# Rotary tables on VectorE, an earlier key for the memory's norm, and products padded to 128 rows

## The chip, the cores and the metric

The kernel runs on one core of one Trainium2 chip. The metric is the device time of one execution in microseconds (us). The median of three runs of the kernel before is 687.25 us (686.97 to 688.6).

## The reference

The reference is a decoder trunk of two layers over one sequence of 256 tokens, 1024 channels wide, in float32. Each layer normalises x, projects it with one matrix (1024 x 8224) and feeds five groups of heads:

- A, sparse attention with eight heads of 64 channels and two key heads: a compressed branch (keys and values of 32 tokens each, one every 16 tokens, so 16 compressed positions), a selected branch and a window branch, merged by gates;
- B, a Mamba-2 scan with eight heads, whose decays are exponentials of differences of running sums;
- C, causal attention in a window of 128, with rotary positions on queries and keys and a learned sink a head;
- D, dilated attention in three patterns;
- M, cross-attention of four heads into 256 memory tokens. The memory is normalised with each layer's own weights.

```python
for layer in range(DEPTH):
    h = rms_norm(x, pre_norm[layer])
    proj = jnp.einsum('bsd,de->bse', h, w_in[layer])
    a_out = nsa_mixer(...)        # compressed values: p_c @ vc, with 16 rows
    b_out = ssd_mixer(...)        # decay = exp(acs[l] - acs[s]) where causal
    c_out, _ = banded_attention(rope(c_q, positions), rope(c_k, positions), c_v, 127, sinks=c_sinks[layer])
    d_out = dilated_mixer(...)
    m_out = memory_attention(m_q, mem, m_norm[layer], m_w_kv[layer])
    mix = jnp.concatenate([a_out * silu(a_z), b_out, c_out * silu(c_z), d_out * silu(d_z), m_out * silu(m_z)], -1)
    x = x + rms_norm(mix @ w_out[layer], post_norm[layer])
```

The rotary angle of a position is the position times 32 inverse frequencies. The kernel builds one table of sines and one of cosines from the positions, once for both layers.

## The kernel before

**Order of the work.** The program records every operation with the tiles it reads and writes, its engine (or two engines to choose from), a cost and a key. The key is the TensorE time that the program has recorded so far plus an offset, in nanoseconds. A list scheduler, `schedule`, then plays the engines forward with these costs: an engine that is free takes the ready operation of the lowest key, if slots for its tiles are free. An operation may be taken up to `HORIZON` (80 us) of keys ahead of the oldest one left, a DMA up to `SP_HORIZON` (30 us). The order that comes out is fixed, each engine works through its own list, and an operation that has no input, such as a memset, can be taken long before its use. Tiles come from classes with fixed numbers of slots: 48 pages (128 x 544, class P), 8 PSUM banks (B), 5 raw weight tiles (R), 4 high and 4 low weight tiles (H and L), 64 small ones (S).

**Numbers.** A float32 operand is split in a high part, rounded to fp32r, and a low part, the difference; a product of two operands takes three fp32r products. A weight tile lands in R by a DMA from SyncE, H is made by ScalarE (or VectorE), L by VectorE (`w_split`). `fm` projects 128 channels in 24 products of 256 columns, `tm` in products of up to 288 columns with tokens on the partitions.

**The start.** The setup runs 34 warming products. Layer 0 then goes through: M's queries and gate paths (four `fm`), A's two projections for compression (`ev_cmp`), the `tm` of 288 columns with A's values, the gates and B's step sizes, and `m_rest`, which calls `mem_kv` (line 1404) for the memory's keys and values. `load_mem` (line 781) loads the memory rows, norms them (`norm_transpose`: squares on ScalarE, a reciprocal root of small VectorE operations, scaled rows, 16 TensorE transposes), and evicts each transposed piece for each layer's norm weights: the high part on ScalarE, the low part on VectorE, eight pieces of two for layer 0 and as many for layer 1. The pages of layer 1 are stored to DRAM by eight DMAs and loaded again at the end of layer 0. For layer 0 the keys of all this begin at the TensorE time recorded so far, that is behind the `tm`; for layer 1 at `-MEM_EARLY`.

**Rotary tables.** `setup_rope` (line 843) runs on GpSimd through two helpers, `pool` (line 497, instructions at L490) and `pool_tt` (line 501, L502), with key 40000. The load of the positions has key 29000. ScalarE computes the sine. The tables are read by `rope` in group C, the last group of a layer.

**Group A.** `cmp_rest` (line 982) makes the compressed keys and values. The values, `vc`, lie on 16 partitions: 64 columns of high part and 64 of low for each key head. `unit_a` (line 1026) runs for four pairs of heads a layer, at background keys (15 us later). It transposes the compressed probabilities into 16 rows of a bank, splits them into pages `ph` and `pl`, and multiplies both with `vc`, into the bank in which the window and selected products then add up.

**Group B.** The running sums of the decays are held in `acsT`, high part in rows 0 to 7 and low part in rows 32 to 39. For each pair of heads TensorE spreads two of the rows over 128 partitions by two products with a column of `pick` (40 rows), and adds the causal mask by a product of 512 columns with the identity.

Of the kernel before, what the change touches and what calls it, by code (L numbers as in the profile page):

```python
# [12 lines left out]
F32 = mybir.dt.float32  # L13
F32R = mybir.dt.float32r
I32 = mybir.dt.int32
AF = mybir.ActivationFunctionType
OP = mybir.AluOpType
# [3 lines left out]
SEQ = 256  # L21
# [27 lines left out]
W_EARLY, DMA_EARLY, T_EARLY, ALT_LATE = 3000.0, 11000.0, 2000.0, 4000.0  # L49
WO_ORDER = [16, 17, 0, 1, 2, 3, 12, 13, 14, 15, 4, 5, 6, 7, 8, 9, 10, 11]  # L50
PSUM = "B"
SOME_LATE, PE_LATE, BIAS_LATE = 40000.0, 6000.0, 3000.0
RESERVE, MEM_EARLY = 1.0, 17000.0
N_WARM, W_KEY = 34, 0.0
# [350 lines left out]
class Trunk(Recorder):  # L405
# [88 lines left out]
        rate = 0.96 if a.buf.cls == PSUM else 1.92  # L494
        self.add({"DVE": self.a_dve((a,), rate, f, s1, s2)}, (a, s1, s2), (out,))

    def pool(self, out, a, s1, op0, s2=None, op1=None):
        fast = (op0, op1) == (OP.mult, OP.add) and not isinstance(s1, V)
        self.add({"POOL": (100 + a.free() * (1.1 if fast else 3.5), self.a_ts(out, a, s1, op0, s2, op1, self.nc.gpsimd))}, (a, s1, s2), (out,))

    def pool_tt(self, out, a, b, op):
        f = lambda: self.nc.gpsimd.tensor_tensor(out=out.ap(), in0=a.ap(), in1=b.ap(), op=op)  # L502
        self.add({"POOL": (100 + a.free() * 2.4, f)}, (a, b), (out,))

    def scale(self, out, a, s, first="DVE"):

        f = self.a_ts(out, a, s, OP.mult, None, None, self.nc.vector)
# [228 lines left out]
    def setup(self):  # L736
        ins = self.ins
        self.offset = W_KEY
        w, b = self.page(F32R), self.bank()
        self.zero(w.v, 1.0)  # L740
        for _ in range(N_WARM):
            self.mm(b[:, 0:512], w[:, 0:128], w[:, 0:512])
        self.pe_time = 0.0
        self.offset = -1e5
        self.cst = self.fixed([128, C_OH], name="cst")
        self.offset = -9e4
        self.dma(self.cst.v, self.cin[:, 0:C_OH])
        self.ident = self.cst[:, C_ID:C_ID + 128]
        self.tri = self.cst[:, C_TRI:C_TRI + 128]
        self.x = self.fixed([128, 2, DM], name="x")  # L750
        nr = self.fixed([32, 128], name="nr")
        self.offset = -1e5
        xs = ins["x"][0].rearrange("(t p) d -> p t d", p=128)
        for t in range(2):
            for j in range(2):
                c = slice(512 * j, 512 * j + 512)
                self.dma(self.x[:, t, c], xs[:, t, c])
        self.offset = -9e4
        for i, n in enumerate(("pre_norm", "m_norm")):
            self.dma(nr[16 * i:16 * i + 16], ins[n].rearrange("l (k p) -> (l k) p", p=128))  # L760
        self.offset = SOME_LATE
        self.ident_r, self.mask_r = (self.fixed([128, 128], F32R, name=n) for n in ("ident_r", "mask_r"))
        self.copy(self.ident_r.v, self.ident)
        self.copy(self.mask_r.v, self.cst[:, C_MASK:C_MASK + 128])
        self.pick = self.fixed([40, 8], F32R, name="pick")
        self.copy(self.pick.v, self.cst[0:40, C_E:C_E + 8])
        self.acsT = self.fixed([40, SEQ], F32R, name="acsT")
        self.zero(self.acsT.v)
        self.ones = self.fixed([128, 128], name="ones")
        self.zero(self.ones.v, 1.0)  # L770
        self.setup_rope()
        self.offset = -8e4
        b = self.bank()
        self.tr(b[:, 0:32], nr.v)
        self.nw = self.fixed([128, 2, 2, KT], name="nw")
        self.cast(self.nw.v, b[:, 0:32].rearrange("p (n l k) -> p n l k", n=2, l=2))
        self.offset = 0.0
        self.hi = self.fixed([128, KT, SEQ], F32R, name="hT_hi")
        self.lo = self.fixed([128, KT, SEQ], F32R, name="hT_lo")
# [63 lines left out]
    def setup_rope(self):  # L843

        self.sc = self.fixed([128, 2, SEQ], name="sincos")
        pi = self.new("P", I32)[:, 0:SEQ]
        off, self.offset = self.offset, SOME_LATE - DMA_EARLY
        self.dma(pi, self.bcast(self.ins["positions"], SEQ))
        self.offset = off
        ang = self.page()[:, 0:SEQ]  # L850
        n, r, u = (self.page()[:, 0:2 * SEQ] for _ in range(3))
        angs = ang[:, None, :].to_broadcast([128, 2, SEQ])
        pair = lambda x: x.rearrange("p (s n) -> p s n", s=2)
        self.pool(ang, pi, self.cst[:, C_INV:C_INV + 1], OP.mult)
        magic = 12582912.0
        c1 = 6.28125
        c2 = float(np.float32(np.round((2 * math.pi - c1) * 2 ** 20) / 2 ** 20))
        c3 = float(np.float32(2 * math.pi - c1 - c2))
        for i in range(2):
            self.pool(n[:, SEQ * i:SEQ * i + SEQ], ang, float(1 / (2 * math.pi)), OP.mult, 0.25 * i, OP.add)  # L860
        for m in (magic, -magic):
            self.pool(n, n, 1.0, OP.mult, m, OP.add)
        for i, c in enumerate((c1, c2, c3)):
            self.pool(u, n, -c, OP.mult, 0.0, OP.add)
            if i:
                self.pool_tt(r, r, u, OP.add)
            else:
                self.pool_tt(pair(r), angs, pair(u), OP.add)
        self.pool(r[:, SEQ:2 * SEQ], r[:, SEQ:2 * SEQ], 1.0, OP.mult, float(math.pi / 2), OP.add)
        self.pool(r, r, 3.1415925, OP.min, -3.1415925, OP.max)  # L870
        self.act(self.sc.v, pair(r), AF.Sin)
        self.pool(self.sc[:, 0], self.sc[:, 0], self.cst[:, C_SGN:C_SGN + 1], OP.mult)
        self.sinT, self.cosT = self.sc[:, 0], self.sc[:, 1]


# [106 lines left out]
    def cmp_rest(self, l, b, kh, kl):  # L982
        hs = self.page()[:, 0:96]
        self.cast(hs, b[:, 0:96])
        u, t = (self.page()[:, 0:64] for i in range(2))
        for kv in range(2):
            self.ts(u[:, 32 * kv:32 * kv + 32], hs[:, 48 * kv:48 * kv + 32], hs[:, 48 * kv + 32:48 * kv + 33], OP.add)
        self.tt(t, u, u, OP.mult)
        self.ts(t, t, 0.044715, OP.mult, 1.0, OP.add)
        self.tt(t, t, u, OP.mult)  # L990
        self.act(t, t, AF.Tanh, scale=math.sqrt(2.0 / math.pi))
        self.stt(u, t, 1.0, u, OP.add, OP.mult)
        b = self.bank()
        self.begin_fuse()
        self.mm(b[0:64, 0:32], self.w2[:, 0, :], u[:, 0:32])
        for g in range(2):
            self.mm(b[0:16, 32 + 64 * g:96 + 64 * g], u[:, 32 + 16 * g:48 + 16 * g], self.w2[:, 1, :])
        self.end_fuse()
        for g in range(2):
            s, vh, vl = b[0:64, 16 * g:16 * g + 16], kh[g][:, 0:16], kl[g][:, 0:16]  # L1000
            self.act(vh[0:64], s, scale=0.5)
            self.act(vh[64:128], s, scale=0.5)
            self.stt(vl[0:64], s, 0.5, vh[0:64].bitcast(F32), OP.mult, OP.subtract)
        vc = self.fixed([16, 2, 128], F32R, name=f"vc{l}").v
        s = b[0:16, 32:160].rearrange("p (g n) -> p g n", g=2)
        self.act(vc[:, :, 0:64], s, scale=0.5)
        self.stt(vc[:, :, 64:128], s, 0.5, vc[:, :, 0:64].bitcast(F32), OP.mult, OP.subtract)
        self.vc = vc

    def k_pages(self, n):  # L1010
# [15 lines left out]
    def unit_a(self, c, q, kh, kl, av, z):  # L1026
        g = c // 2
# [6 lines left out]
        for par in range(2):  # L1034
            h = 2 * c + par
# [29 lines left out]
        pv = None  # L1065
        blocks = (None, [(0, 0, 0), (1, 0, 0)], [(0, 0, 1), (0, 1, 1)], [(1, 0, 1), (1, 1, 1)])
        for n, bl in enumerate(blocks):
            bt = self.bank()
            m = 16 if bl is None else 128
            self.begin_fuse()  # L1070
            if bl is None:
                for t in range(2):
# [6 lines left out]
                        o = 256 * i + 128 * par  # L1079
                        self.tr(bt[:, o:o + 128], src(t, br, kb, par))  # L1080
            self.end_fuse()
            ph, pl = self.page(F32R), self.page(F32R)
            self.split(ph[0:m, 0:512], pl[0:m, 0:512], bt[0:m, :])
            if bl is None:
                pv = self.bank()
                self.begin_fuse()
                self.mm(pv[:, :], self.vc[:, g, :], ph[0:16, 0:512], start=True, stop=False)
                self.mm(pv[:, :], self.vc[:, g, :], pl[0:16, 0:512], start=False, stop=False)
                self.end_fuse()
            else:  # L1090
                self.begin_fuse()
                for i, (br, kb, t) in enumerate(bl):
                    o = pv[:, 256 * t:256 * t + 256]
# [213 lines left out]
    def ssd(self, l, pre, XY, zz):  # L1307
# [43 lines left out]
        for g in range(2):  # L1351
            for p in range(2):
# [2 lines left out]
                self.begin_fuse()  # L1355
                for i in range(2):
                    h = 4 * g + 2 * p + i
                    self.mm(v[:, i], self.pick[:, h:h + 1].to_broadcast([40, 128]), self.acsT.v, start=(i == 0), stop=False)
                self.mm(b.v, self.ident_r.v, self.mask_r[:, None, :].to_broadcast([128, 4, 128]), start=False, stop=True)
                self.end_fuse()  # L1360
                for t in range(2):
# [41 lines left out]

    def mem_kv(self, l, after=None):
        mkv = self.ins["m_w_kv"][l]
        self.offset = 0.0 if after is None else -MEM_EARLY
        mem = self.load_mem(l)
        self.after, self.offset = after, 0.0
        ks = [self.ev_k(self.fm(mem, (mkv, 128 * c, 128))) for c in range(2)]
# [190 lines left out]
```

## Time and profile before

| | |
|---|---|
| median of three runs | 687.25 us |
| the profiled execution: time, span | 687.48 us, 685.7 us |
| mean granted TensorE clock | 0.987 |
| TensorE (PE) products busy | 668.2 us (97%), 5051 |
| VectorE (DVE) busy | 615.9 us (90%) |
| ScalarE (ACT) busy | 491.5 us (72%) |
| GpSimd (POOL) busy | 32.8 us (5%) |
| DMA | 114.28 MB, mean 167 GB/s |

How to read it: PE is TensorE's products, PEld its weight loads, DVE VectorE, ACT ScalarE, POOL GpSimd, SP SyncE, which issues DMAs. A product's recorded duration is longer than its step, the time from its start to the start of the next, since products are pipelined; what a product costs is read from the steps. PEclk is the granted TensorE clock as a share of its full speed. L456 is the line of the helper that issues products, L462 transposes, L468 ScalarE operations, L485 two-input VectorE operations, L518 those with a scalar and a tensor, L490 operations with a scalar on VectorE or GpSimd. In a tile's name, P, B, R, H, L and S are the classes above.

### The profile page before, as it was taken

To read this page: it belongs to the slowest core of one execution; us is meant where nothing else is said; L and a number is where in the kernel's file an instruction comes from. 1 tells how busy PE (TensorE), PEld (TensorE's weight loads), DVE (VectorE), ACT (ScalarE), POOL (GpSimd) and SP (SyncE) were. 2 spreads that over 40 slices of the span, in tenths; PEclk is the share of its full clock that TensorE was granted. 3 is DMA by queue.
4 is the path that set the end of the run, shared out by engine and by line. 5 is a ranking of instruction groups with operands and counts; after the bars stand their busy time and mean duration, and the time that the engine had idled before them with its cause. 6 is when DMAs were issued, how large, how long until landed. Compare 5 with 4: busy or idle time off the path is not lost.

```text
span 685.7 us, 14368 instructions
## 1 busy us (share of the span) xinstructions
PE 668.2 (97%) x5051; PEld 628.3 (92%) x5051; DVE 615.9 (90%) x1777; ACT 491.5 (72%) x1230; POOL 32.8 (5%) x78
## 2 busy tenths in 40 slices
PE   8889999999999999999999999999999999999995
PEld 7879999999999998988889999899999999898884
DVE  5959899999999999998688889999999899999875
ACT  6465679997875878676476469989678677768541
POOL 2520000000000200100000000000000000000000
PEclk9978999999999999999999999999999999999998
DMA  8999652648685656545538973185967534753511
GB/s 218 253 246 277 171 152 63 185 132 233 175 227 156 180 146 199 155 124 184 159 94 234 251 202 93 32 212 140 273 158 200 164 86 125 213 154 124 171 45 62
DMA packets 163536, 114.28 MB, mean 167 GB/s; under 512 B 8694, under 2 KB 154760, under 8 KB 163464
## 3 DMA queue, kind: packets, MB, share of 16 engines
q1 hardware_dynamic: 162312, 111.26, 58.3%
q0 software_dynamic: 1152, 2.10, 1.2%
q8 instruction: 40, 0.66, 0.4%
q14 instruction: 32, 0.26, 0.1%
HBM read 110.14 MB, written 3.20 MB: 165 GB/s over the span
## 4 chain that ended last, share of the span: by engine, by line
PE 72%; DVE 17%; ACT 8%; issue 2%; DMA 0%; DVEq 0%; POOL 0%; SPq 0%; ACTq 0%; POOLq 0%
PE B L456 68%; ACT P L468 6%; PE B L462 4%; DVE P L485 4%; DVE L L485 4%; DVE P L518 3%; DVE P L522 2%; ACT H L468 2%; DVE S L518 1%; DVE P L490 1%; DVE hT_lo L518 1%; DVE x L518 0%; DVE S L490 0%; ACT L468 0%; DVE H L556 0%
## 5 line engine op out<-in xcount | busy, mean ns | idle before, releaser
L485 DVE TENSOR_TENSOR L<-R,H 128x1024 fp32r<-128x1024 f32 (+1 forms) x174 | 210.1, 1217 | 22.3 <-ACT H L468 20.1
L468 ACT ACTIVATE P<-B 64x256 fp32r<-64x256 f32 (+9 forms) x404 | 158.7, 404 | 69.6 <-PE B L456 46.0
L468 ACT ACTIVATE H<-R 128x1024 fp32r<-128x1024 f32 (+1 forms) x150 | 156.5, 1052 | 66.5 <-PE B L456 49.9
L468 ACT ACTIVATE P<-P,S 128x256 f32<-128x256 f32 (+5 forms) x262 | 112.4, 449 | 38.1 <-DVE S L531 18.2
L456 PE MATMUL B<-hT_hi,L 128*128 128x256 f32 x864 | 128.2, 284 | 3.3 <-DVE L L485 3.3
L456 PE MATMUL B<-P,P 128*128 128x256 f32 (+6 forms) x896 | 125.8, 279 | 0.7 <-DVE P L485 0.6
L456 PE MATMUL B<-hT_hi,H 128*128 128x256 f32 x864 | 124.3, 282 | 0.6 <-ACT H L468 0.6
L456 PE MATMUL B<-hT_lo,H 128*128 128x256 f32 x864 | 124.4, 281 | 0.0
L456 PEld LDWEIGHTS B<-P,P 128*128 128x128 f32 (+1 forms) x896 | 113.0, 184 | 6.0 <-ACT P L468 2.1
L456 PEld LDWEIGHTS B<-hT_hi,L 128*128 128x128 f32 x864 | 112.0, 190 | 3.8 <-DVE L L485 3.6
L456 PEld LDWEIGHTS B<-hT_hi,H 128*128 128x128 f32 x864 | 110.7, 188 | 1.8 <-ACT H L468 0.8
L456 PEld LDWEIGHTS B<-hT_lo,H 128*128 128x128 f32 x864 | 110.8, 188 | 0.1
L456 PE MATMUL B<-H,P 128*128 128x512 f32 (+1 forms) x352 | 103.3, 377 | 0.0
L485 DVE TENSOR_TENSOR P<-B,P 64x256 f32<-64x256 f32 (+5 forms) x186 | 91.6, 508 | 13.0 <-ACT P L468 10.3
L456 PEld LDWEIGHTS B<-H,P 128*128 128x128 f32 x352 | 62.1, 188 | 9.9
L456 PE MATMUL B<-L,P 128*128 128x512 f32 (+1 forms) x176 | 65.7, 373 | 0.0
L522 DVE CUSTOM_DVE_ANT_0 P<-B,P 128x128 f32<-128x128 f32 (+2 forms) x192 | 52.5, 320 | 0.6
L462 PE MATMUL B<-cst,P 128*128 128x128 f32 (+1 forms) x344 | 50.2, 276 | 1.3 <-ACT P L468 0.6
L456 PE MATMUL B<-H,hT_hi 128*128 128x256 f32 (+1 forms) x160 | 46.3, 289 | 0.0
L456 PE MATMUL B<-L,hT_hi 128*128 128x256 f32 (+1 forms) x160 | 46.2, 289 | 0.0
L456 PE MATMUL B<-H,hT_lo 128*128 128x256 f32 (+1 forms) x160 | 46.1, 288 | 0.0
L462 PEld LDWEIGHTS B<-cst,P 128*128 128x128 f32 (+1 forms) x344 | 38.3, 136 | 7.3 <-ACT P L468 2.7
(127 smaller groups left out, 703.4 us busy)
## 6 DMA issues: line engine op xcount, KB each, us to landing
R<-in_w_in_dram SPq DMA_DIRECT2D x124, 512.0 KB, 4.8
R<-in_w_out_dram SPq DMA_DIRECT2D x36, 512.0 KB, 3.8
P<-scr SPq DMA_DIRECT2D x64, 136.0 KB, 4.8
R<-in_m_w_kv_dram SPq DMA_DIRECT2D x8, 512.0 KB, 4.8
P<-in_a_cmp_w_dram SPq DMA_DIRECT2D x16, 256.0 KB, 4.8
mem_d<-P SPq DMA_DIRECT2D x8, 256.0 KB, 3.2
P<-mem_d POOLq DMA_DIRECT2D x8, 256.0 KB, 4.3
x<-in_x_dram SPq DMA_DIRECT2D x4, 256.0 KB, 3.9
```

What stands on the lines that cost most here:

```text
L456: f = lambda: self.nc.tensor.matmul(out=out.ap(), lhsT=lhsT.ap(), rhs=rhs.ap(), start=start, stop=stop)
L462: f = lambda: self.nc.tensor.transpose(out.ap(), in_.ap(), idn.ap())
L468: f = lambda: self.nc.scalar.activation(out=out.ap(), in_=in_.ap(), func=func, **{k: _ap(x) for k, x in kw.items()})
L485: f = lambda: self.nc.vector.tensor_tensor(out=out.ap(), in0=a.ap(), in1=b.ap(), op=op)
L490: return lambda: eng.tensor_scalar(out.ap(), a.ap(), _ap(s1), _ap(s2), **kw)
L518: f = lambda: self.nc.vector.scalar_tensor_tensor(out=out.ap(), in0=a.ap(), scalar=_ap(s), in1=b.ap(), op0=op0, op1=op1)
L522: f = lambda: self.nc.vector.tensor_tensor_reduce(out=out.ap(), in0=a.ap(), in1=b.ap(), scale=1.0, scalar=3e38, op0=OP.add, op1=OP.min, ac ...
```

## The change

- `setup_rope` issues its operations on VectorE, as eleven instead of fourteen: the two-input forms multiply and add in one. All its operations, the positions' load among them, have key 80000 (`ROPE_LATE`). The helpers `pool` and `pool_tt` go.
- For layer 0 `mem_kv` sets the offset `-MEM0_EARLY`, 6 us, for all of `load_mem`: loads, norm, transposes, evictions, stores.
- `pick` and `acsT` have 128 rows instead of 40, with zeros in the rows that are not used.
- `vc` has 128 rows, zeroed, with the same values in rows 0 to 15 and 32 to 47. In `unit_a` the compressed probabilities' high part goes to rows 0 to 15 and the low part to rows 32 to 47 of one zeroed page; one product takes the place of two.

```diff
+ROPE_LATE, MEM0_EARLY = 80000.0, 6000.0
...
-        self.pick = self.fixed([40, 8], F32R, name="pick")
-        self.copy(self.pick.v, self.cst[0:40, C_E:C_E + 8])
-        self.acsT = self.fixed([40, SEQ], F32R, name="acsT")
+        self.pick = self.fixed([128, 8], F32R, name="pick")
+        self.copy(self.pick.v, self.cst[:, C_E:C_E + 8])
+        self.acsT = self.fixed([128, SEQ], F32R, name="acsT")
...
+        self.offset = ROPE_LATE
         self.setup_rope()
...
-        off, self.offset = self.offset, SOME_LATE - DMA_EARLY
         self.dma(pi, self.bcast(self.ins["positions"], SEQ))
-        self.offset = off
...
-        self.pool(ang, pi, self.cst[:, C_INV:C_INV + 1], OP.mult)
+        self.ts(ang, pi, self.cst[:, C_INV:C_INV + 1], OP.mult)
...
-            self.pool(n[:, SEQ * i:SEQ * i + SEQ], ang, float(1 / (2 * math.pi)), OP.mult, 0.25 * i, OP.add)
+            self.ts(n[:, SEQ * i:SEQ * i + SEQ], ang, float(1 / (2 * math.pi)), OP.mult, 0.25 * i, OP.add)
         for m in (magic, -magic):
-            self.pool(n, n, 1.0, OP.mult, m, OP.add)
-        for i, c in enumerate((c1, c2, c3)):
-            self.pool(u, n, -c, OP.mult, 0.0, OP.add)
-            if i:
-                self.pool_tt(r, r, u, OP.add)
-            else:
-                self.pool_tt(pair(r), angs, pair(u), OP.add)
-        self.pool(r[:, SEQ:2 * SEQ], r[:, SEQ:2 * SEQ], 1.0, OP.mult, float(math.pi / 2), OP.add)
-        self.pool(r, r, 3.1415925, OP.min, -3.1415925, OP.max)
+            self.ts(n, n, m, OP.add)
+        self.stt(pair(r), pair(n), -c1, ang[:, None, :].to_broadcast([128, 2, SEQ]), OP.mult, OP.add)
+        for c in (c2, c3):
+            self.stt(r, n, -c, r, OP.mult, OP.add)
+        self.ts(r[:, SEQ:2 * SEQ], r[:, SEQ:2 * SEQ], float(math.pi / 2), OP.add)
+        self.ts(r, r, 3.1415925, OP.min, -3.1415925, OP.max)
         self.act(self.sc.v, pair(r), AF.Sin)
-        self.pool(self.sc[:, 0], self.sc[:, 0], self.cst[:, C_SGN:C_SGN + 1], OP.mult)
+        self.ts(self.sc[:, 0], self.sc[:, 0], self.cst[:, C_SGN:C_SGN + 1], OP.mult)
...
-        vc = self.fixed([16, 2, 128], F32R, name=f"vc{l}").v
+        vc = self.fixed([128, 2, 128], F32R, name=f"vc{l}").v
+        self.zero(vc)
         s = b[0:16, 32:160].rearrange("p (g n) -> p g n", g=2)
-        self.act(vc[:, :, 0:64], s, scale=0.5)
-        self.stt(vc[:, :, 64:128], s, 0.5, vc[:, :, 0:64].bitcast(F32), OP.mult, OP.subtract)
+        for o in (0, 32):
+            self.act(vc[o:o + 16, :, 0:64], s, scale=0.5)
+        for o in (0, 32):
+            self.stt(vc[o:o + 16, :, 64:128], s, 0.5, vc[0:16, :, 0:64].bitcast(F32), OP.mult, OP.subtract)
...
-            ph, pl = self.page(F32R), self.page(F32R)
-            self.split(ph[0:m, 0:512], pl[0:m, 0:512], bt[0:m, :])
+            ph = self.page(F32R)
             if bl is None:
+                self.zero(ph[:, 0:512])
+                self.split(ph[0:16, 0:512], ph[32:48, 0:512], bt[0:16, :])
                 pv = self.bank()
-                self.mm(pv[:, :], self.vc[:, g, :], ph[0:16, 0:512], start=True, stop=False)
-                self.mm(pv[:, :], self.vc[:, g, :], pl[0:16, 0:512], start=False, stop=False)
+                self.mm(pv[:, :], self.vc[:, g, :], ph[:, 0:512], start=True, stop=False)
             else:
+                pl = self.page(F32R)
+                self.split(ph[:, 0:512], pl[:, 0:512], bt[:, :])
...
-                    self.mm(v[:, i], self.pick[:, h:h + 1].to_broadcast([40, 128]), self.acsT.v, start=(i == 0), stop=False)
+                    self.mm(v[:, i], self.pick[:, h:h + 1].to_broadcast([128, 128]), self.acsT.v, start=(i == 0), stop=False)
...
-        self.offset = 0.0 if after is None else -MEM_EARLY
+        self.offset = -MEM0_EARLY if after is None else -MEM_EARLY
```

## Rows read from the trace of the kernel before

**Rows 1.** The page: busy us (share) and instructions of each engine.

```profile
PE 668.2 (97%) x5051; PEld 628.3 (92%) x5051; DVE 615.9 (90%) x1777; ACT 491.5 (72%) x1230; POOL 32.8 (5%) x78
```

**Rows 2.** Windows: length, busy us of each engine, PEclk, DMA share, GB/s.

```profile
20.00:30.00 10.00, 10.00 (x88) 10.00 (x87) 9.64 (x29) 6.98 (x17) 5.00 (x8) 1.00 0.96 243
30.00:40.00 10.00, 7.15 (x33) 6.54 (x33) 8.43 (x9) 4.30 (x10) 7.51 (x8) 0.66 0.95 266
40.00:45.00 5.00, 5.00 (x42) 5.00 (x42) 1.02 (x2) 1.76 (x3) 0.00 (x0) 1.00 1.16 309
45.00:60.00 15.00, 12.49 (x67) 10.24 (x66) 12.03 (x26) 12.94 (x29) 1.59 (x4) 0.77 0.82 240
60.00:300.00 240.00, 239.67 (x1974) 231.98 (x1973) 229.89 (x704) 187.87 (x490) 10.14 (x23) 1.00 0.62 169
300.00:346.00 46.00, 45.80 (x240) 38.37 (x239) 35.89 (x82) 23.77 (x50) 0.68 (x8) 1.00 0.52 161
```

**Rows 3.** TensorE in order of time: start, us, operation, count [idle before].

```profile
24.57 1.10 PE L456 MATMUL B<-hT_hi,L 128*128 128x256 f32 x8
25.51 1.10 PE L456 MATMUL B<-hT_hi,H 128*128 128x256 f32 x8
...
332.27 0.63 PE L456 MATMUL B<-H,P 128*128 128x512 f32 x2
332.74 0.39 PE L456 MATMUL B<-L,P 128*128 128x512 f32 x1
```

**Rows 4.** TensorE in order of time, its waits at the start.

```profile
33.19 1.22 PE L456 MATMUL B<-hT_hi,L 128*128 128x256 f32 x4 [2.85 <-DVE L L485]
...
47.73 2.77 PE L456 MATMUL B<-P,H 128*128 128x256 f32 x7 [1.24 <-ACT P L468]
51.77 2.48 PE L456 MATMUL B<-P,H 128*128 128x256 f32 x9 [1.26 <-ACT P L468]
```

**Rows 5.** VectorE and GpSimd in order of time, 28 to 33 us.

```profile
28.57 2.38 DVE L490 TENSOR_SCALAR P<-P,S 128x512 f32<-128x512 f32 x2
30.87 2.27 DVE L485 TENSOR_TENSOR L<-R,H 128x1024 fp32r<-128x1024 f32 x1
...
28.61 1.29 POOL L502 TENSOR_TENSOR P<-P,P 128x512 f32<-128x512 f32 x1
```

**Rows 6.** VectorE's groups by shape: count, busy us, mean ns, idle before.

```profile
L485 DVE TENSOR_TENSOR L<-R,H 128x1024 fp32r<-128x1024 f32 x168 | 204.6, 1225 | 21.0 <-ACT H L468 18.8 <-ACT P L468 1.5
...
L490 DVE TENSOR_SCALAR P<-P,S 128x256 f32<-128x256 f32 x43 | 14.1, 349 | 0.0
...
L518 DVE SCALAR_TENSOR_TENSOR P<-P,P 128x512 f32<-128x512 f32 x12 | 8.3, 689 | 0.0
...
L490 DVE TENSOR_SCALAR P<-x,S 128x512 f32<-128x512 f32 x3 | 1.5, 486 | 0.1
```

**Rows 7.** ScalarE and VectorE in order of time, 43 to 55 us.

```profile
43.61 1.28 ACT L468 ACT_TABLE_LOAD   x1
...
47.20 4.51 ACT L468 ACTIVATE P<-B,nw 128x256 fp32r<-128x256 f32 x12
...
48.82 5.79 DVE L518 SCALAR_TENSOR_TENSOR P<-B,nw,P 128x256 fp32r<-128x256 f32 x14
```

**Rows 8.** TensorE in order of time, around products with vc and pick.

```profile
109.43 0.63 PE L456 MATMUL B<-hT_hi,L 128*128 128x256 f32 x4
109.98 0.73 PE L456 MATMUL B<-P,vc 16*128 16x512 f32 x2
110.64 1.80 PE L456 MATMUL B<-P,P 128*128 128x256 f32 x13
...
257.73 0.63 PE L456 MATMUL B<-hT_lo,H 128*128 128x256 f32 x4
258.28 0.50 PE L456 MATMUL B<-acsT,pick 40*128 40x256 f32 x2
...
259.06 0.62 PE L456 MATMUL B<-hT_lo,H 128*128 128x256 f32 x4
```

More of the change, by code (lines that the diff above doesn't have):

```diff
@@ L495, in ts @@
         self.add({"DVE": self.a_dve((a,), rate, f, s1, s2)}, (a, s1, s2), (out,))
[L497 to L503, printed above, removed]
     def scale(self, out, a, s, first="DVE"):
@@ L846, in setup_rope @@
         pi = self.new("P", I32)[:, 0:SEQ]
-        off, self.offset = self.offset, SOME_LATE - DMA_EARLY
         self.dma(pi, self.bcast(self.ins["positions"], SEQ))
-        self.offset = off
         ang = self.page()[:, 0:SEQ]
-        n, r, u = (self.page()[:, 0:2 * SEQ] for _ in range(3))
-        angs = ang[:, None, :].to_broadcast([128, 2, SEQ])
+        n, r = (self.page()[:, 0:2 * SEQ] for _ in range(2))
         pair = lambda x: x.rearrange("p (s n) -> p s n", s=2)
-        self.pool(ang, pi, self.cst[:, C_INV:C_INV + 1], OP.mult)
+        self.ts(ang, pi, self.cst[:, C_INV:C_INV + 1], OP.mult)
         magic = 12582912.0
@@ L1068, in unit_a @@
             bt = self.bank()
-            m = 16 if bl is None else 128
             self.begin_fuse()
@@ L1081, in unit_a @@
             self.end_fuse()
-            ph, pl = self.page(F32R), self.page(F32R)
-            self.split(ph[0:m, 0:512], pl[0:m, 0:512], bt[0:m, :])
+            ph = self.page(F32R)
             if bl is None:
+                self.zero(ph[:, 0:512])
+                self.split(ph[0:16, 0:512], ph[32:48, 0:512], bt[0:16, :])
                 pv = self.bank()
-                self.begin_fuse()
-                self.mm(pv[:, :], self.vc[:, g, :], ph[0:16, 0:512], start=True, stop=False)
-                self.mm(pv[:, :], self.vc[:, g, :], pl[0:16, 0:512], start=False, stop=False)
-                self.end_fuse()
-            else:
+                self.mm(pv[:, :], self.vc[:, g, :], ph[:, 0:512], start=True, stop=False)
+            else:
+                pl = self.page(F32R)
+                self.split(ph[:, 0:512], pl[:, 0:512], bt[:, :])
                 self.begin_fuse()
```

## The prediction

> **What bounds the kernel now.** I read the page's busy shares first, then the windows, the order of time on each engine at the start, and last the groups by shape. TensorE is busy for 668.2 of 685.7 us and VectorE for 615.9 [rows 1]: two engines are near full, so each stretch has to be asked which of them holds it.
>
> From 60 to 300 us TensorE is idle for 0.33 us of 240, and VectorE for 10.1 us [rows 2]. TensorE sets the pace there and VectorE follows closely. TensorE's own step from product to product, where nothing waits, is 0.117 us for 256 columns (eight in 0.94) and 0.235 us for 512 (two in 0.47) [rows 3].
>
> The start is another matter. From 20 to 60 us three things cost time [rows 2, 4]. TensorE waits 2.85 us until 33.19 for VectorE's L, the low half of a weight tile, and 1.24 and 1.26 us before 47.73 and 51.77 for ScalarE's P, the normalised memory. After each place the granted clock lies lower: a mean of 0.66 over 30 to 40 us is 6.8 us at the lower of the two levels (1.2 and 2.4 GHz), and 0.77 over 45 to 60 us is 6.9 us. If the clock fell towards the end of the first wait, some 0.7 us of the first stretch and 1.3 us of the second are idle (an estimate), so 6.1 and 5.6 us of work ran at half speed and lost 3.05 and 2.8 us. The seven products from 47.73 took 2.77 us where 0.82 would do, of which I count 1.3 us as slow feeding, not clock. In all 5.35 + 5.85 + 1.3 = 12.5 us hang on the start.
>
> **The change part by part.** My sum is made on the profiled execution, 687.48 us, of which 685.7 us are its span; the median of the three runs is 687.25.
>
> *Padding on TensorE.* A unit of group A has two products of 16 rows and 512 columns with vc. Four steps of 0.117 from 109.43 end at 109.90, but the first product starts at 109.98: 0.08 us. The two last 0.66 us until 110.64. The thirteen behind them take 1.80 us where 12 x 0.117 + 0.28 = 1.68 would do (0.28 us is what the last of eight shows: 1.10 - 7 x 0.117): 0.12 us [rows 3, 8]. Together 0.86 us. One product of 128 rows, high and low parts stacked, replaces them at 0.235: 0.63 us less, in eight units 5.0 us. For pick, four steps from 257.73 end at 258.20 and the first product starts at 258.28 (0.08 us); the three then last 0.78 us until 259.06. With 128 rows they would take 2 x 0.117 + 0.235 = 0.47: 0.39 us less, in eight groups 3.1 us. Sum: 8.1 us, half in each layer, on the engine that sets the pace. From below: if padded products cost what the 16-row ones do, only eight of 0.33 us go, 2.6 us. I take 8.1, since neighbours with 128 rows show the low price in the same microsecond. What is added lies elsewhere: ten memsets on GpSimd, which is idle for 230 of 240 us in that stretch [rows 2] and has no input to wait for; and per layer one short ScalarE and one short VectorE operation more for vc, at most a 256-column operation's 0.35 us [rows 6]. If a memset came late, the copy that fills the page would wait for it with TensorE's product behind it, once per unit. The low parts need no page of their own any more, but the zeroed page is held from its memset on.
>
> The Trainium skill ("TensorE: Matmul & The Clock Gate", "Why this matters for your kernels") says that a single matmul with a contraction of 32 takes as long as one with 128. By that rule only the halving would count. The rows speak against it here, with 0.33 us for a 16-row step against 0.235 us; no row has the padded form itself.
>
> *Rope off GpSimd.* The tables run on GpSimd, 12.5 us of 20 to 40 us, among them sums over 512 columns at 1.29 us [rows 2, 5]. Beside them VectorE slows down: two scalings of 128x512 take 2.38 us, where the same shape elsewhere takes 0.486 each (1.41 us more), and the L at 30.87 takes 2.27 us against a mean of 1.225 (1.05 us more) [rows 5, 6]. Exactly this L is what TensorE waits for. The two excesses, 2.46 us, are most of the wait of 2.85 us, and with the small operations before them, slowed too, I count the wait as gone, and with it the 3.05 us of low clock. What comes late next is the 864-column L for the next projection, which follows on VectorE at once; its input lands early enough as the transfers run now.
>
> *The tables on VectorE under the later key.* Eleven operations: five over 256 columns at 0.35, three scalings over 512 at 0.486, three two-input ones over 512 at 0.689 [rows 6]: 1.75 + 1.46 + 2.07 = 5.3 us. From below, short of the fixed part, I see 3 us; above, at the stretched 1.03 us a scaling, 8. They fall due at 60 to 90 us, where VectorE is 96% busy. Their consumer, group C, comes after 230 us, so the chain itself is never awaited. The sine and two loads of function tables, with little else, fill ScalarE from 43.61 to 47.20 [rows 7] straight ahead of the memory's scalings; they move out of that place, at the same price, to one where ScalarE has more than a fifth idle. The positions' load moves with them on SP's queue, so nothing behind it waits longer than now.
>
> *The memory's norm under the earlier key.* By the program's order TensorE's 16 transposes of the memory come after the 288-column projection now; 6 us earlier they come at its beginning. The scalings, sixteen on ScalarE (twelve take 4.51 us) and sixteen on VectorE (fourteen take 5.79 us) [rows 7], then run beside that projection, in a stretch where VectorE works 1.0 and ScalarE 1.8 of 5 us [rows 2]. The two waits of 1.24 and 1.26 us and the second low clock, 2.8 us, go if this holds. The eight stores of the second layer's memory come earlier on SP too, past weight loads that are queued behind them.
>
> *What the start gives.* Not all 12.5 us, because of the transfers: from 20 to 60 us they move 2.43 + 2.66 + 1.55 + 3.60 = 10.2 MB, and the busiest row shows 309 GB/s [rows 2]. At that rate 10.2 MB last 33 us, so 7 us come out of 40; a little more if the stores slip behind. I take 7.5 us, between 2 (another wait in their place) and 12.5.
>
> *What VectorE gives back.* From 60 to 300 us it has 10.1 us idle. It gets 5.3 + 0.35 us more to do, and TensorE's work there shrinks by 4.05: 229.9 + 5.65 = 235.5 us of work in 236 us. That can't all hold. Between 0 (the lag is made up from 300 to 346 us, where VectorE has 10.1 us idle and TensorE has output products to do [rows 2]) and 5.65 + 4.05 = 9.7 us (nothing is made up), I take 3 us, nearer to the first, as TensorE can run those products while it waits for group C.
>
> Sum: 687.48 - 8.1 - 7.5 + 3 = 674.9, said as 675.
>
> **The rivals.**
>
> *A wait stays at the start, and a low clock with it.* The transfers, or the memory's 32 scalings ahead of the weight splits in ScalarE's and VectorE's queues, make TensorE wait once more. For it: the start's transfers are near their busiest rate. Against: ScalarE and VectorE have room at 40 to 45 us. The start gives 3 in place of 7.5: 679.5.
>
> *The start loses all its waits, and VectorE's lag is hidden.* For it: VectorE's idle time behind 300 us. Against: the 10.2 MB. 687.5 - 8.1 - 12.5 + 0.5 = 667.5.
>
> *The padding gains only the halving*, as by the rule above: 2.6 in place of 8.1, 680.4.
>
> *Slower: VectorE, not TensorE, sets the end of each layer.* Its sum changes by +5.65 for the tables and vc, and by -3.3 for what GpSimd no longer slows (1.41 + 1.05 and some 0.8 of small operations): +2.3 us, 689.8, while all that TensorE saves turns into waiting. It decides from the point where less than some 2 us of VectorE's 10.1 idle us can be used. Against it: TensorE's 0.33 idle us of 240.
>
> *Pages run out.* Four zeroed pages a layer are held for long ahead of their use, the tables' now later. If group A's units wait for pages, TensorE idles with a low clock behind it; two such places, 6 us each, and nothing from the start: 687.5 - 8.1 + 12 = 691. The profile shows no sign of it.
>
> **How the numbers follow.** My forecast has 0.46; a wait that stays 0.20; all waits gone 0.17; only the halving 0.06; VectorE as the bound 0.07; pages 0.04. The range reaches from 667 (all waits gone) to 684 (a wait that stays, with VectorE giving back 7 us), and leaves out the two slow cases and a little below. What can be told from no change is 0.3%, 2 us: under 685.2 is faster. The first four cases are, save 0.01 at their upper edge: 0.88. Of the other two 0.07 is slower and 0.04 falls between: 0.05 the same, 0.07 slower.
>
> **What would show it.** Padding: steps of 0.117 and 0.235 us at the pick and vc products, no gap before or after, eight vc products in place of sixteen. Rope: nothing of L490 or L502 on GpSimd, the L before the 288-column projection at 1.2 us, no wait near 30 us, a clock of 1.00 there. Memory: the 16 transposes ahead of most of the 288-column products, no wait before the memory's projection. VectorE's share of 60 to 300 us near 98% and TensorE's steps there still 0.117 us: right; steps that stretch or waits for VectorE's P or L there: the giving back is larger. The forecast is wrong if the low clock shows up elsewhere, or if TensorE's idle time in the middle grows over 5 us.

## The result and the profile after

The changed kernel takes 681.0 us (median of four runs, 680.3 to 681.5) against 687.9 (687.0 to 688.7): a ratio of 0.990 [0.988, 0.992], 6.9 us less. Forecast were 12.5 us on the profiled execution. The profiled execution after took 681.53 us, 5.95 us less than the one before (687.48); its span is 679.7 us.

The page after, busy us (share) and instructions of each engine, as [rows 1]:

```profile
PE 660.7 (97%) x5043; PEld 625.1 (92%) x5043; DVE 615.2 (91%) x1784; ACT 496.3 (73%) x1238; POOL 23.8 (4%) x74
```

The windows after, with the columns of [rows 2]:

```profile
20.00:30.00 10.00, 10.00 (x88) 10.00 (x87) 9.16 (x31) 8.11 (x18) 1.19 (x4) 1.00 0.92 252
30.00:40.00 10.00, 10.00 (x78) 9.51 (x76) 7.69 (x15) 8.38 (x22) 0.14 (x2) 1.00 1.12 307
40.00:45.00 5.00, 5.00 (x36) 4.13 (x36) 5.00 (x12) 4.95 (x15) 0.00 (x0) 1.00 1.14 325
45.00:60.00 15.00, 15.00 (x131) 15.00 (x130) 13.51 (x40) 6.34 (x13) 1.05 (x2) 1.00 1.03 306
60.00:300.00 240.00, 233.87 (x1897) 226.81 (x1896) 229.75 (x699) 194.71 (x493) 9.78 (x23) 0.99 0.61 166
300.00:346.00 46.00, 45.87 (x233) 38.15 (x232) 34.46 (x81) 23.83 (x50) 2.62 (x12) 1.00 0.52 156
```

From 20 to 60 us TensorE is never idle and its clock stays at 2.4 GHz (1.00); GpSimd has 2.4 us there in place of 14.1. From 60 to 300 us the opposite has happened: TensorE, idle for 0.33 us before, is idle for 6.1, and the clock's mean is no longer 1.00.

Where the time went, from the starts of three products in both traces: the first product of 128x48 at the end of the start, the first one of layer 1, the last with w_out. TensorE has done the same work by each of them (359 products by the first, in both).

| stretch, us | before | after | change | forecast |
|---|---|---|---|---|
| to the first 128x48 product | 64.62 | 52.72 | -11.9 | -7.5 |
| from there to layer 1 (layer 0) | 301.23 | 308.03 | +6.8 | -4.05 + 3 |
| layer 1 to the last w_out product | 311.70 | 310.79 | -0.9 | -4.05 |

The start in TensorE's order of time (start, us, operation, count):

```profile
30.33 1.09 PE L457 MATMUL B<-hT_hi,L 128*128 128x256 f32 x8
34.08 1.25 PE L463 MATMUL B<-cst,P 128*128 128x128 f32 x10
40.22 0.75 PE L457 MATMUL B<-P,H 128*128 128x256 f32 x4
41.68 1.69 PE L457 MATMUL B<-P,H 128*128 128x256 f32 x12
```

and VectorE's:

```profile
27.91 0.81 DVE L491 TENSOR_SCALAR P<-P,S 128x512 f32<-128x512 f32 x1
28.65 1.21 DVE L486 TENSOR_TENSOR L<-R,H 128x1024 fp32r<-128x1024 f32 x1
36.85 5.00 DVE L511 SCALAR_TENSOR_TENSOR P<-B,nw,P 128x256 fp32r<-128x256 f32 x12
```

The L that TensorE waited for took 1.21 us in place of 2.27 [rows 5]; the transposes of the memory (L463) stand at 34 us, and its projection from 40.22 meets no wait (TensorE is busy for all of 40 to 60 us). [Rows 4] has nothing left.

The new loss lies at 94 to 108 us. TensorE there:

```profile
94.32 1.20 PE L457 MATMUL B<-hT_hi,H 128*128 128x256 f32 x8
95.36 1.10 PE L457 MATMUL B<-hT_lo,H 128*128 128x256 f32 x8
96.30 0.40 PE L457 MATMUL B<-P,P 128*128 128x256 f32 x2
101.98 1.22 PE L457 MATMUL B<-hT_hi,L 128*128 128x256 f32 x4 [5.29 <-DVE L L486]
```

ScalarE:

```profile
85.76 1.06 ACT L469 ACTIVATE H<-R 128x1024 fp32r<-128x1024 f32 x1 [0.82 <-ACT P L469]
...
94.92 1.28 ACT L469 ACT_TABLE_LOAD   x1
96.22 0.63 ACT L469 ACTIVATE sincos<-P 128x512 f32<-128x512 f32 x1
96.86 1.28 ACT L469 ACT_TABLE_LOAD   x1
98.16 0.30 ACT L469 ACTIVATE P<-P,S 128x8 f32<-128x8 f32 x1
...
100.01 0.49 ACT L469 ACTIVATE P<-P,S 128x256 f32<-128x256 f32 x1
```

VectorE:

```profile
96.88 0.35 DVE L491 TENSOR_SCALAR sincos<-sincos,cst 128x256 f32<-128x256 f32 x1 [1.13 <-ACT sincos L469]
97.57 1.27 DVE L491 TENSOR_SCALAR P<-P,S 128x8 f32<-128x8 f32 x6
100.63 0.17 DVE L491 TENSOR_SCALAR S<-S 128x6 f32<-128x6 f32 x1 [1.46 <-ACT P L469]
100.71 1.22 DVE L486 TENSOR_TENSOR L<-R,H 128x1024 fp32r<-128x1024 f32 x1
```

Read the last line backwards. The L at 100.71 needs the H of 85.76, done since 86.8: its input is not what it waits for. It stands in VectorE's queue behind the tables' last scaling, which waits 1.13 us for the sine, and behind a step of group A that waits 1.46 us for exponentials; these stand in ScalarE's queue behind the second load of a function table. TensorE waits 5.29 us at the end of this chain. The window around it:

```profile
100.00:112.00 12.00, 10.02 (x61) 9.68 (x62) 9.63 (x37) 10.12 (x35) 0.52 (x1) 0.72 0.35 88
```

A mean of 0.72 over 12 us is 6.7 us at 1.2 GHz. Slices of 2 us put them at 100.9 to 107.8, so 1.1 us are idle time and 5.8 us of work lost 2.9. Wait and clock are 8.2 us.

The padded products, in TensorE's order:

```profile
110.48 0.28 PE L457 MATMUL B<-H,hT_lo 128*128 128x256 f32 x1
110.60 0.40 PE L457 MATMUL B<-P,vc 128*128 128x512 f32 x1
110.83 0.63 PE L457 MATMUL B<-P,P 128*128 128x256 f32 x4
...
255.36 0.40 PE L457 MATMUL B<-acsT,pick 128*128 128x256 f32 x2
255.59 0.39 PE L457 MATMUL B<-mask_r,ident_r 128*128 128x512 f32 x1
255.82 0.63 PE L457 MATMUL B<-hT_hi,L 128*128 128x256 f32 x4
...
456.13 0.63 PE L457 MATMUL B<-hT_hi,H 128*128 128x256 f32 x4
457.37 0.48 PE L457 MATMUL B<-P,vc 128*128 128x512 f32 x1 [0.61 <-DVE P L486]
457.69 0.94 PE L457 MATMUL B<-P,P 128*128 128x256 f32 x4
```

The pick group takes 0.46 us to the next product's start (0.47 forecast). The vc product at 110.60 takes 0.23, with no gap on either side, as forecast; the one at 457.37 waits 0.61 us for VectorE's half of its page and then takes 0.32.

### The profile page after: what moved, and what is told of

Same layout as the page of the kernel before. It is cut to its first block, busy times and chain, and to the rows that moved or that the text cites. A ratio compares the mean times of both kernels' runs of the same rounds, so it can differ in the third digit from the quotient of the medians.

```text
span 679.7 us, 14371 instructions
## 1 busy us (share of the span) xinstructions
PE 660.7 (97%) x5043; PEld 625.1 (92%) x5043; DVE 615.2 (91%) x1784; ACT 496.3 (73%) x1238; POOL 23.8 (4%) x74
## 4 chain that ended last, share of the span: by engine, by line
PE 69%; DVE 19%; ACT 9%; issue 2%; DVEq 0%; POOL 0%; ACTq 0%; POOLq 0%
PE B L457 65%; ACT P L469 6%; DVE P L486 5%; PE B L463 4%; DVE L L486 4%; DVE P L511 3%; DVE P L515 2%; ACT H L469 1%; DVE P L491 1%; DVE S L511 1%; DVE H L549 0%; DVE x L511 0%; DVE S L491 0%; ACT L469 0%; DVE hT_lo L511 0%
## 5 line engine op out<-in xcount | busy, mean ns | idle before, releaser
L469 ACT ACTIVATE P<-B 64x256 fp32r<-64x256 f32 (+10 forms) x405 | 159.3, 404 | 61.2 <-PE B L457 40.4
L469 ACT ACTIVATE H<-R 128x1024 fp32r<-128x1024 f32 (+1 forms) x155 | 161.1, 1049 | 57.4 <-PE B L457 37.7
L457 PE MATMUL B<-P,P 128*128 128x256 f32 (+6 forms) x896 | 128.7, 280 | 0.4 <-DVE P L486 0.2
L457 PEld LDWEIGHTS B<-P,P 128*128 128x128 f32 (+1 forms) x896 | 114.6, 184 | 4.6 <-DVE P L486 1.5
L463 PE MATMUL B<-cst,P 128*128 128x128 f32 (+1 forms) x344 | 51.0, 282 | 1.8 <-ACT P L469 0.8
L463 PEld LDWEIGHTS B<-cst,P 128*128 128x128 f32 (+1 forms) x344 | 39.4, 140 | 7.8 <-ACT P L469 2.5
```

What stands on the lines that cost most here:

```text
L457: f = lambda: self.nc.tensor.matmul(out=out.ap(), lhsT=lhsT.ap(), rhs=rhs.ap(), start=start, stop=stop)
L463: f = lambda: self.nc.tensor.transpose(out.ap(), in_.ap(), idn.ap())
L469: f = lambda: self.nc.scalar.activation(out=out.ap(), in_=in_.ap(), func=func, **{k: _ap(x) for k, x in kw.items()})
```

## The experiments

The runs stand in three groups (e1 to e4, e5 to e8, e9 to e12), each timed beside the kernel before on its own chip; ratios are to that. Its medians there are 687.6, 688.7 and 688.5 us.

**e1 and e6: the changed kernel without the two table loads.** The same edit twice; it leaves the order of the operations on every engine as it was, and the tables hold wrong values.

```diff
-        self.act(self.sc.v, pair(r), AF.Sin)
+        self.act(self.sc.v, pair(r), AF.Tanh)
```

> The changed kernel with the sine's function replaced by the hyperbolic tangent, which shares its function table with the exponential: the tables hold wrong values, every engine's order is that of the changed kernel, and only ScalarE's two loads of function tables (1.28 us each) around it are gone. Changed kernel: 681.0 us, one wait of TensorE of 5.3 us until 102 us, low clock behind it. Theory (the loads stand in ScalarE's queue between the exponentials of group A, VectorE waits for these, and the weight tile's low part waits behind in VectorE's queue): the wait falls under 2.5 us, the clock stays 1.00, and 681 - 5.3 - 3 gives about 673 to 675. Rival 1 (the tables' eleven operations on VectorE hold the low part up): at most the 2.6 us of the loads go, the wait stays over 2.5 us with its low clock, 678 to 680. Rival 2 (TensorE has merely run ahead of VectorE, which would make it wait there anyway): within 1 us of 681.

e1: 678.9 us, 0.990 [0.984, 0.995]. The interval is too wide to tell it from the changed kernel. In its trace the wait is 2.5 us in place of 5.29, no low clock follows, and layer 0 lasts 303.1 us in place of 308.0; its start held a wait of 1.6 us that the other had not.

**e5 and e6: the changed kernel and e1's edit again, side by side in five rounds.**

> The changed kernel, for a comparison with the next three on one chip: about 7 us under the kernel before, one wait of 5 us near 100 us with low clock behind it.

> Again the sine's function replaced by the hyperbolic tangent (wrong tables, no loads of function tables around it, the same order on every engine). The first run's trace had a wait of 2.5 us left at 98 us and no low clock, and layer 0 from its first compression product to layer 1's first product 4.9 us shorter. Theory (the two loads, 2.6 us, give back twice their length, by the wait and by the clock): 4 to 6 us under the changed kernel. Rival (what was given back there returns as other waits): within 2 us of it.

e5: 680.6 us, 0.989 [0.987, 0.991]. e6: 679.3, 0.987 [0.985, 0.989]. TensorE in e6, the same place:

```profile
97.55 0.40 PE L457 MATMUL B<-P,P 128*128 128x256 f32 x2
100.46 0.73 PE L457 MATMUL B<-hT_hi,L 128*128 128x256 f32 x4 [2.51 <-DVE L L486]
```

e5 waits 5.27 us there. Layer 0 is 302.9 us in e6 and 306.6 in e5, 3.6 less; e6's start is 1.4 us longer in the profiled execution. So the loads make half of the wait, and the medians, 1.3 us apart with intervals that overlap, missed the 4 to 6 us that I had expected and lie where the rival had them. The other half stays without them. The windows of 95 to 100 us, after and then e6:

```profile
95.00:100.00 5.00, 1.70 (x15) 1.49 (x13) 3.04 (x20) 4.96 (x13) 0.00 (x0) 1.00 0.01 3
95.00:100.00 5.00, 2.95 (x23) 2.56 (x21) 5.00 (x30) 5.00 (x20) 0.00 (x0) 1.00 0.01 3
```

With the loads VectorE (DVE, the third busy time) stands still for 2.0 of the 5 us; without them it never does, and TensorE still waits 2.51 us. That half is VectorE's own queue.

**e2: the padding alone**, on the kernel before: the change's lines for pick, acsT and vc.

> The kernel before with the padding alone (pick, running sums, compressed values and probabilities on 128 rows). Theory: the eight groups of vc give 0.63 us each and those of pick 0.39, all on TensorE, which sets the pace: 687.9 - 8.1 = 679.8, with the start's waits near 33, 47 and 52 us as in the kernel before. Rival (padding is worth only the product saved): 685.3. Rival (VectorE sets the end): 687 to 688, with TensorE's waits grown in the middle.

685.6 us, 0.997 [0.995, 0.9999]. Its trace has layer 0 in 299.2 us (301.2 before) and layer 1 in 310.9 (311.7): 2.9 us in all, where 8.1 was forecast. The time is near the rival's 685.3, but the steps are not the rival's: a pick group takes 0.46 us here too, and a vc product without a wait 0.24.

**e3: the tables alone on VectorE, e4: the memory's key alone**, both on the kernel before.

```diff
+ROPE_LATE = 80000.0            # e3, with the new setup_rope
+        self.offset = ROPE_LATE
+MEM0_EARLY = 6000.0            # e4
-        self.offset = 0.0 if after is None else -MEM_EARLY
+        self.offset = -MEM0_EARLY if after is None else -MEM_EARLY
```

> The kernel before with the rotary tables on VectorE under the key 80000, and nothing else. Theory (GpSimd slows VectorE at the start, and the sine's loads hold up the memory's scalings): the wait of 2.85 us at 33 us goes with its low clock, 5.9 us, and the waits at 47 and 52 us shrink; near 90 to 100 us the sine's loads cost again what they cost in the changed kernel, some 5 to 8 us. Sum 681 to 688. Rival (the wait at 33 us came from the order, not from GpSimd): the wait stays over 1.5 us, 688 to 694.

> The kernel before with the memory's norm 6 us earlier in keys, and nothing else. Theory: the tables on GpSimd still slow VectorE, so the wait near 33 us stays or grows, with its low clock; the waits at 47 and 52 us go with theirs: 687.9 - 2.5 - 2.8 - 1.3 = 681.3. Rival (the memory's scalings run into the slowed VectorE and the wait only moves): 686 to 690.

e3: 685.1 us, 0.998 [0.995, 1.001]. e4: 683.3, 0.995 [0.992, 0.998]. TensorE in e3, then VectorE and TensorE in e4:

```profile
43.67 2.53 PE L457 MATMUL B<-P,H 128*128 128x256 f32 x10 [1.20 <-ACT P L469]
```

```profile
30.61 2.35 DVE L491 TENSOR_SCALAR P<-P,S 128x512 f32<-128x512 f32 x2
32.89 2.27 DVE L486 TENSOR_TENSOR L<-R,H 128x1024 fp32r<-128x1024 f32 x1
```

```profile
35.22 1.01 PE L457 MATMUL B<-hT_hi,L 128*128 128x256 f32 x3 [3.93 <-DVE L L486]
```

Without GpSimd's work (e3) the wait near 33 us is gone and one for the memory is left. With GpSimd's work and the earlier memory (e4) the memory's waits are gone, VectorE's L takes 2.27 us still, and the first wait grows from 2.85 to 3.93 us (in its profiled execution, 685.1 us, which is 1.8 us above its median). Each half of the start has its own cause, and each part of the change removes its own. In the traces the start ends at 56.3 (e3), 60.5 (e4) and 52.7 us with both. Behind it, layer 0 (301.2 us before) lasts 307.3 us in e3, with small waits of TensorE near 100 us and no low clock: 6.1 us more with the tables alone. In e4 it lasts 302.8.

**e7: the loads known to the planner; e8: the same, and the tables earlier; e9: the tables earlier alone.**

```diff
-        c = ... + self.part((in_, out))                                   # e7, e8
+        c = ... + self.part((in_, out)) + (2566 if func == AF.Sin else 0)
-ROPE_LATE, MEM0_EARLY = 80000.0, 6000.0                                   # e8, e9
+ROPE_LATE, MEM0_EARLY = 50000.0, 6000.0
```

> The changed kernel with 2566 ns more cost for the sine in the scheduler's plan, so that the order allows for the two loads that ScalarE has to make; nothing else. Theory (the wait comes from an order that did not know of the loads): the low part is made ahead of the waiting operations, the wait near 100 us falls under 2.5 us, and the time is 3 to 6 us under the changed kernel. Rival (VectorE has no room there whatever the order): within 1.5 us of the changed kernel, with the wait or a row of small ones in its place.

> As the last one, and the rotary tables' key 50000 in place of 80000. The tables fall due at some 45 to 65 us, where ScalarE is busy for 6.3 of 15 us and VectorE for 13.5 of 15. Theory: the sine's loads meet no exponentials of group A, no wait over 1.5 us from 60 to 110 us, 4 to 7 us under the changed kernel. Rival (VectorE's eleven operations then hold up the weight tiles behind the memory's projection): a wait of 2 us or more at 50 to 65 us with a low clock, 0 to 4 us over the changed kernel.

> The changed kernel with the rotary tables' key 50000 in place of 80000, and the sine's cost as it was. Theory (the place decides, not the plan's knowledge of the loads): within 2 us of the run that had both, 0.978 of the kernel before, no wait over 1.5 us from 60 to 110 us. Rival (the plan's cost mattered there): a wait of 2 us or more behind the sine, 677 to 682.

e7: 679.6 us, 0.988 [0.986, 0.989]: no low clock, but waits of 2.2, 0.7 and 0.6 us between 96 and 108 us, as its rival had it; with the loads planned for, VectorE's queue still has no room there (busy for 11.94 of the 12 us). e8: 673.2, 0.978 [0.977, 0.980], the shortest time of all kernels run. e9: 675.1, 0.981 [0.978, 0.983], with no wait over 0.6 us from 60 to 300 us. ScalarE in e8, then the windows of e8:

```profile
58.40 1.28 ACT L469 ACT_TABLE_LOAD   x1
60.87 0.63 ACT L469 ACTIVATE sincos<-P 128x512 f32<-128x512 f32 x1 [1.19 <-DVE P L491]
62.62 0.77 ACT L469 ACTIVATE P<-B 64x256 fp32r<-64x256 f32 x2 [1.12 <-PE B L457]
63.41 1.28 ACT L469 ACT_TABLE_LOAD   x1
```

```profile
20.00:110.00 90.00, 89.74 (x748) 87.35 (x747) 85.43 (x280) 73.19 (x199) 3.43 (x10) 1.00 0.77 212
60.00:300.00 240.00, 237.82 (x1934) 229.75 (x1933) 232.46 (x695) 196.78 (x510) 10.05 (x25) 1.00 0.63 170
```

The same loads, the same sine and the same VectorE operations, with keys 30 us earlier: ScalarE even has idle time around them, and TensorE is busy for all but 0.26 us from 20 to 110 us. Layer 0 is 300.6 us in e8 and 301.6 in e9, where the padding alone has 299.2. So against the padding alone layer 0 is 1.4 to 2.4 us longer with the tables in a place with room, and 8.9 in the one that they were given. These figures have the memory's earlier key in them, which lengthens layer 0 by 1.6 us by itself (e4); the runs don't tell how much of each is its.

**e10 and e11: is the padding's gain held back by VectorE?** The kernel before (e10) and e2's kernel (e11), in which VectorE's in-place scalings and the convolution's multiply-adds touch 8 columns in place of all.

```diff
-                self.stt(d, r[:, k:k + 256], cw[:, k, ch:ch + 1], d, OP.mult, OP.add)
+                self.stt(d, r[:, k:k + 256], cw[:, k, ch:ch + 1], d, OP.mult, OP.add, True)
```

> The kernel before in its own order, but VectorE's in-place scalings of probabilities and the convolution's multiply-adds touch 8 columns alone (the rest stays unscaled): some 40 us of VectorE's 616 go, most of them between 80 and 300 us and at the same place in layer 1. It is the base of the next run. If VectorE held TensorE up in the kernel before, it falls by more than 3 us; if TensorE set the pace, by under 3.

> The same with the padding. The padding alone gave 2 to 3 us of the 8.1 that TensorE's steps promised. Theory (VectorE, near full, took the rest back): with VectorE relieved the padding gives 6 to 8 us against the relieved base. Rival (the order that comes with the padding takes it back, with the product that now waits for both halves of the split): still 2 to 4 us, with waits before the vc products of 0.3 to 0.8 us in layer 1.

e10: 686.9 us, 0.996 [0.994, 0.999], though VectorE is busy for 599.2 us in place of 615.9 (16.7 us less, not the 40 expected): before the change these 16.7 us set little of the time. e11: 680.0, 0.988 [0.985, 0.991]. From the first 128x48 product to the last with w_out the padding gives 4.65 us with VectorE relieved (611.34 to 606.69) and 2.86 without (612.93 to 610.07). By medians it is 6.8 and 1.9 (e2), but the executions differ in their mean granted clock; those of e10 and e11 with a like clock are 4.7 (0.986 to 0.988) and 5.2 us apart (0.991 to 0.993), near the trace's 4.65. VectorE holds back a part of the gain; whether it holds back more, this relief of 16.7 us can't show.

**e12: e8 with each unit's compressed branch last**, so that the vc product has 12 products more ahead of it.

```diff
-        blocks = (None, [(0, 0, 0), (1, 0, 0)], [(0, 0, 1), (0, 1, 1)], [(1, 0, 1), (1, 1, 1)])
+        blocks = ([(0, 0, 0), (1, 0, 0)], [(0, 0, 1), (0, 1, 1)], [(1, 0, 1), (1, 1, 1)], None)
```

> The kernel of key 50000 with the sine's loads in the plan, and in each unit of group A the compressed branch's transposes, split and product come last instead of first, so that the split has the other branches' products in front of it. Theory (the padded product waits because its one page takes both halves of the split and nothing of the unit is ready ahead of it): the waits of 0.3 to 0.8 us before it go, 1 to 3 us under that kernel's 673. Rival (the waits belong to VectorE and only move to the unit's end, where the merge follows the product): within 1 us of 673, or over it.

674.8 us, 0.980 [0.978, 0.982]. The time lost ahead of the eight vc products (from the start of the product before each, less that one's 0.117 us) falls from 1.8 us in e8 to 0.05, but layer 1 lasts 310.5 us in both, and the kernel is not faster than e8. The rival came out: what went there turned up elsewhere.

## Why the prediction was right and wrong

**Right: the start and its two causes.** Sums over 512 columns on GpSimd beside VectorE made the L late; e3 takes them away, with the rest of the tables, and the wait goes; e4 leaves them and it grows. The memory's transposes and scalings beside the 288-column projection take the other waits away.

**Mis-sized: the start's 7.5 us.** It gave 11.9, near the 12.5 that I had counted as hanging on it. The cap by transfers was the wrong step: I took the bytes moved from 20 us on as needed by the same place in the work, and 309 GB/s as the most. From 20 us to the first 128x48 product the traces have 11.3 MB before and 9.7 after; the changed kernel gets there at 52.72 us with transfers at 252 to 325 GB/s and no wait for one. A part of those bytes was for later work.

**Wrong: "to one where ScalarE has more than a fifth idle".** I gave the sine and its two loads the price of nothing there, and asked of VectorE only how many us it had to do. The shares were means of 60 to 300 us, the 96% that I gave VectorE for 60 to 90 us among them. In the kernel before, 60 to 90 and 90 to 120 us read, with the columns of [rows 2]:

```profile
60.00:90.00 30.00, 30.00 (x263) 30.00 (x262) 26.98 (x76) 18.67 (x45) 1.04 (x2) 1.00 0.65 180
90.00:120.00 30.00, 30.00 (x252) 29.09 (x251) 29.25 (x130) 25.24 (x90) 0.52 (x1) 1.00 0.42 110
```

VectorE is busy for 26.98 us of the first 30 and for 29.25 of the second 30, where the sine came to stand. A mean of idle time over 240 us says nothing about one place. Around 95 us group A's exponentials run on ScalarE with steps of VectorE between them, and the next weight tile's L is queued behind those. 3.2 us put ahead of the exponentials went through both queues to TensorE; the clock fell during the wait. Against the padding alone, layer 0 is 8.9 us longer: 5.3 of wait, 2.9 of clock, 0.7 spread over the rest, where 3 us were forecast as what VectorE gives back. e1 and e6 give the loads half of the wait, and the clock's fall went with it; the other half is VectorE's own queue. e8 and e9 show that the place decides, since with keys 30 us earlier the same layer is 1.4 to 2.4 us longer, not 8.9. The Trainium skill ("ScalarE: Activation LUTs", "What ACT_TABLE_LOAD costs") has some 1283 ns for a load, and a drain of some 1380 ns more for each switch. The trace agrees on the load, 1.28 us, but shows no drain: ScalarE stands for 0.02 us on either side of a load. What it adds is that the load is a price on the engines queued behind, not only on ScalarE. The eleven operations themselves cost no more than said: the two-input ones 0.69 us each.

**Wrong: the 8.1 us of the padding.** The direct prices hold: 0.46 us for a pick group, 0.23 for a vc product that doesn't wait. By the rule of the Trainium skill that the prediction weighed ("TensorE: Matmul & The Clock Gate", "Why this matters for your kernels") a single product of few rows takes as long as one with 128. The traces don't bear it out for a step among 128-row products: 0.33 us with 16 rows, 0.23 with 128. What failed is that eight vc units save 0.63 us each. Before, gaps (0.8 us), pairs (5.25) and what followed slowly (1.0) were 7.0 us; after, eight products take 2.35 us and the time lost ahead of and behind them is 2.2: 2.5 saved, not 5.0. Before, the product with the high part could start while VectorE made the low part; the stacked product needs both. I named the wait for a late memset as the danger, and overlooked the wait for the split's slower half. But a kernel without this wait is not shown to be shorter: e12 takes it away and gains nothing. With pick's 3.1 that leaves 5.6 us, of which e2 shows 2.9. Some 1.8 us come back when VectorE is relieved (e11 against e10); the last us stays open. "VectorE as the bound" was thus right in part as a mechanism, though far from its price of 689.8.

The sum closes: -11.9 + 8.9 - 2.9 = -5.9, against -6.0 from trace to trace at the last w_out product. That the time fell into the range is in part luck: 4.4 us more at the start stood against 11 us less elsewhere. The place of the loss was none of the rivals'. The prediction named two signs that would make it wrong, a low clock that shows up elsewhere and over 5 us of TensorE's idle time in the middle; both came, the second with 6.1 us.

## What to carry to other kernels

Where work is moved, read the order of time at its new place on every engine that it touches, and ask what is queued behind it there and who waits for that; a mean of idle time over a long stretch can't answer. A pair of products fused into one waits for the later of its two inputs, and taking that wait away gains nothing where, as in e12, the time turns up elsewhere: ask which engine makes the input and how much room it has. Transfers of a stretch aren't all needed in it, so a bound from their bytes can be too tight.

## What was not expected of the hardware

- The clock after a wait isn't told by the wait's length alone. 2.85 us before, 3.93 (e4) and 5.29 us are followed or joined by some 6.8 us at 1.2 GHz, e5's 5.27 us by about 3.5 (a mean of 0.92 over 90 to 112 us), e6's 2.51 us by none, e1's 1.63 us at 28 to 30 us by none, and e3's 1.20 us again by some 3.5 (0.92 over 40 to 45 and 0.91 over 45 to 60 us).
- A padded vc product takes 0.30 to 0.34 us to the next one's start in five units of e8 and 0.23 to 0.24 in three. In e8 the five are those with time lost ahead of them, but in e12 three take 0.34 with at most 0.02 us lost ahead; the cause stays open.
- Beside GpSimd's sums a scaling of 128x512 on VectorE took 1.18 us (e4: two in 2.35); without them 0.81 at 27.91 us (beside a memset of 0.52 us on GpSimd at 27.92), still more than the 0.486 of [rows 6]; in e3, with nothing on GpSimd beside it, 0.49 at 28.04 us.
